# Four edits to a two-branch encoder layer: gated copies, 2 KB rows for an intermediate, an engine pinned for some splits, and attention scores in runs of four blocks

## The chip, the cores and the metric

The kernel runs on 1 core of one Trainium2 chip. The metric is the device time of one execution in microseconds, taken over several executions. One core has five instruction streams: TensorE (PE in the profile; its weight loads are PEld), VectorE (DVE), ScalarE (ACT), GpSimd (POOL) and SyncE (SP), which here issues every DMA. All DMAs of this kernel go through SyncE's one queue and are carried out by 16 DMA engines. On chip there are SBUF (128 partitions) and PSUM (eight banks of 128 x 512 float32, which TensorE writes and VectorE and ScalarE read).

## What is computed

One encoder layer is applied to two inputs, a prompt of 512 tokens and a sample of 1024 tokens, with shared weights; the model width is 1024.

```python
h = rmsnorm(x, norm_g)
qa, ka, va, za, qb, kb, vb, zb, ga, gb = split(h @ w_in)       # 1024 x 5376
oa = neighbourhood_attention(norm(qa), norm(ka), va, rpb_a) * silu(za)   # branch A: 8 heads of 64, 8 x 16 window on a grid 64 wide
oa = oa @ w_o_a                                                # 512 x 1024
ob = window_gqa_attention(norm(qb), norm(kb), vb, t5_table, sink_b) * silu(zb)  # branch B: 8 heads, 2 key heads, |i-j| <= 128
ob = ob @ w_o_b
y = x + (sigmoid(ga) * oa + sigmoid(gb) * ob) @ w_out
```

Everything is float32. The kernel keeps that accuracy by splitting each operand of a matmul into a high part (rounded to the matrix engine's float32 format) and a low part (the difference), and by adding three products: high x high, high x low, low x high. ScalarE makes a high part by a copy; VectorE or GpSimd makes the low part by a subtraction.

## The kernel before

**Stages.** First comes the prompt's attention (`attention_phase`), then the prompt's dense phase (`dense_phase`: the gates z and g, the two projections back to width 1024, the merge, the output), then the same two for the sample. Within the trace the prompt's attention lies at about 10 to 215 us, its dense phase up to about 395, the sample's attention from there to about 786, the sample's dense phase after that.

**Order of the work.** Nothing is ordered by hand. Every instruction or small group is an `Op` of the class `Flow`, with a list of engines that may do it and an assumed duration on each, a priority `prio` (smaller is earlier), values that it makes, uses or fills (`new`, `use`, `into`, `hold`), and other operations that it comes after. `Flow.run` is a list scheduler in Python that simulates the engines with the assumed durations while the program is built, and emits instructions in the order in which it would start them. Each engine then works through its own fixed stream on the chip. An operation that has both VectorE and GpSimd among its choices goes to the one that would end it first, and is marked `port`: the planner doesn't start a marked operation on one of the two engines while a marked one runs on the other. An operation with VectorE alone is not marked unless it says so. A DMA is assumed to take 470 ns of SyncE's queue and then a time by its bytes. A value belongs to a rotation of `bufs` buffers, and a new one waits until the oldest is free. `f.begun[nt, prio]` is the first matmul of the projection with that priority.

**Attention.** The heads are done in six groups: branch A as four groups of two heads (`gi` 0 to 3), branch B as two groups of four query heads and one key head. Priorities rise by one for each tile of 128 tokens: the projection of tile `t` in group `gi` has `prio = gi * nb + t`, with `nb` = 4 tiles for the prompt and 8 for the sample. `project` (L764) makes 384 columns of q, k, v of one tile by 24 matmuls into a PSUM bank of the two with the tag `p`; the squares' sums (`ss`, VectorE), the reciprocal root (`rs_v` and `rs_r`, GpSimd) and the scaled q and k (`qk`, VectorE) follow, then TensorE transposes `qk` (L864) and ScalarE and VectorE write `kt` and `qt`. For branch B the rows of h are first copied to the buffers `hb` in natural order of tokens (L665 and L667, four copies of 128 x 512 a tile, on ScalarE or VectorE; four buffers, so one tile's copies are in flight at a time).

`attend` (L937) computes scores. It takes a batch of blocks of 128 queries, two blocks for branch A and one for branch B, and gives each block's head a whole PSUM bank of the five with the tag `x`. A pair of heads lies on partitions 0 to 63 and 64 to 127, so score matmuls use 64 rows of the array each. In the prompt a block of branch A has 256 keys. Prompt's four blocks of branch A cover tiles (0, 1), (1, 2), (2, 3) and, for both ends of the sequence, (0, 3). `weigh` then adds the bias and takes the maximum on VectorE (L972), the exponential on ScalarE (L981), scales, transposes on TensorE (L1029), splits into `pp` (L1035, L1040), multiplies by `v` (L1066) and stores the outcome `ot`. The rotation of `v` has six buffers for the prompt.

A block's outcome goes to the DRAM tensor `o_d`. For branch B the block's 128 queries are every `nb`-th column of h's order, so `post_z` reads `o_d` back in pieces: for a half of 512 columns of the sample, 128 partitions x 8 blocks x 64 columns, 256 bytes a piece.

**Fill-in.** `fill_gates` takes some gate products (weights `fr`, split into `fh` and `fl`, PSUM bank with the tag `d`) at a late priority, so that TensorE has work where attention has none ready.

**Dense phase of the sample.** Most products of two pairs of weight chunks with two halves of h are done by a scheme with seven products instead of eight (`pair_strassen`), which multiplies sums of weights (`S`) with sums of h. h's sums are made early, stored in DRAM as `t_d`, and read back by `stored_sums` at the start of the phase into `U`, `fh` and `w32`, from which `split` makes the high and low parts `T` (L1172 on ScalarE, L1177 on VectorE or GpSimd). L1293 to L1295 are the three products. `post_z` multiplies silu(z) with what attention left; its loads are L1535, the store of the result `u_d` is L1520.

Of the kernel before, what the change touches and what calls it, by code (L numbers as in the profile page):

```python
# [10 lines left out]
F32 = mybir.dt.float32  # L11
# [15 lines left out]
SLACK = 1.1  # L27
SCRATCH = 1024
# [12 lines left out]
P = 128  # L41
# [313 lines left out]
def encoder_kernel(  # L355
# [23 lines left out]
    nc = tc.nc  # L379
# [24 lines left out]
    o_d = {geo.nt: dpool.tile([2, 8, P, geo.nt], F32, tag=f"o_d{geo.nt}", name=f"o_d{geo.nt}") for geo in (gp, gs)}  # L404
# [246 lines left out]
    def attention_phase(geo, hh, hl, h_ops, mask_d, early, late):  # L651
# [79 lines left out]
        def project(br, w, t, prio):  # L731
# [10 lines left out]
            else:  # L742
# [6 lines left out]
                for q in range(2):  # L749
                    for m, v in enumerate((hh, hl)):  # L750
# [5 lines left out]
                            prio - 1, new=[hb[m][q]], hold=[v], after=[o for u in h_ops.values() for o in u], port=True,  # L756
# [154 lines left out]
        def attend(br, gi, g, batch, nb_t, info, prio):  # L911

            nh = 2 if br == "A" else 4
            k0 = 2 * (gi % 2)
            states = []
            for block in batch:
                sums = tuple(tile_([P, 4], F32, tag, 3) for tag in ("mx", "sm", "rs", "es"))
                pss = [bank("x") for _ in range(nh)]
# [7 lines left out]
            def emit(e):  # L926

                for block, _, pss, _ in states:
                    runs, tiles, width, step, whole = places(block)
                    q = queries(block)  # L930
                    for pair in range(nh // 2):
                        at = runs[0][0] if whole else pair * P
                        for n, (u, k) in enumerate(((0, 0), (0, 1), (1, 0))):
                            for i in range(2):
                                rows = slice(64 * i, 64 * i + 64)
                                kv = kt.t[rows, k0 + k].rearrange("p (t n) -> p t n", n=P)
                                pe.matmul(  # L937
                                    pss[2 * pair + i].t[:, :width], q.t[rows, u, at : at + P],
# [3 lines left out]
            def queries(block):  # L942
# [5 lines left out]
                (("pe", ns),), emit, prio, new=[v for _, _, pss, sbs in states for v in (*pss, *sbs)],  # L948
# [12 lines left out]
        def weigh(br, gi, g, block, sums, pss, sbs, nb_t, info, prio):  # L961
# [7 lines left out]
            def score(i, ps, sb):  # L969
                def emit(e, i=i, ps=ps, sb=sb):  # L970
                    init = 3.0e38 if br == "A" else nsink[:, 4 * g + i : 4 * g + i + 1]
                    dve.tensor_tensor_reduce(  # L972
                        out=sb.t[:, :width], in0=ps.t[:, :width], in1=bias_of(br, nb_t, i, table), scale=1.0,
# [18 lines left out]
            for i, (ps, sb) in enumerate(zip(pss, sbs)):  # L992
                score(i, ps, sb)
# [82 lines left out]
            if br == "A":  # L1076
# [10 lines left out]
                def emit():  # L1087
                    if len(runs) == 1:
                        dst = over(o_d[nt][0, g], runs).rearrange("(i p) n -> p i n", i=2)
                        nc.sync.dma_start(dst, ot.t[:64, ::2])  # L1090
                        return
                    for i in range(2):
                        dst = over(o_d[nt][0, g, 64 * i : 64 * i + 64], runs)
# [3 lines left out]
            else:  # L1097
                for e in range(2):
                    dst = o_d[nt][e, 4 + 2 * g : 6 + 2 * g, :, runs[0][0] : runs[0][0] + P]
                    dst = dst.rearrange("c (i d) n -> d (c i) n", d=64)  # L1100
                    o = sp(
                        lambda e=e, dst=dst: nc.sync.dma_start(dst, ot.t[e * 64 : e * 64 + 64]),
                        131072, prio, use=[ot],
                    )
                    for c in (4 + 2 * g, 5 + 2 * g):
# [848 lines left out]
```

## Time and profile before

| | us |
|---|---|
| median of 3 runs | 1133.49 |
| lowest, highest | 1132.47, 1138.85 |
| profiled execution | 1135.29 |
| its span, first to last instruction | 1133.5 |
| TensorE busy | 1119.0 (99%) |
| VectorE busy | 860.1 (76%) |
| ScalarE busy | 651.9 (58%) |
| GpSimd busy | 337.3 (30%) |

Busy time of TensorE counts an instruction from its start to its modelled end, and matmuls overlap in the pipeline: a busy TensorE can still be slower than it might be. The rows of the profile name an instruction by engine, line of the kernel, and out<-in with the program's tile names (`w` stands for `w32`). All times of rows are from the span's start.

### The profile page before, as it was taken

How to read it: one execution, taken by the hardware profiler on the slowest of the kernel's cores; microseconds unless marked ns; L12 is line 12 of the kernel's file. 1: busy time of each engine (PE TensorE's matmuls, PEld its weight loads, DVE VectorE, ACT ScalarE, POOL GpSimd, SP SyncE). 2: the span in 40 equal slices, each digit the busy share in tenths (PEclk: the TensorE clock that was granted, in tenths of full speed). 3: DMA queues.
4: the chain of work that ended last, by engine and by line, in shares of the span. 5: the costliest groups of instructions: out<-in, count | busy, mean ns of one | idle time of the engine just before them, and what ended most of it. 6: DMA issues, size and time to landing. Idle time of an engine off the chain costs nothing.

```text
span 1133.5 us, 18690 instructions
## 1 busy us (share of the span) xinstructions
PE 1119.0 (99%) x6079; PEld 973.2 (86%) x6079; DVE 860.1 (76%) x1988; ACT 651.9 (58%) x1499; POOL 337.3 (30%) x438
## 2 busy tenths in 40 slices
PE   8999999999999999999999999999999999999998
PEld 6999988888888889999999988988788888888887
DVE  5888797587776568787878888885988766677764
ACT  6777987644432257565769888876543335423430
POOL 4653433000011154434324344420333322222211
PEclk9999999999999999999999999999999999999999
DMA  7854543488886732121212314244977645867862
GB/s 263 276 155 138 184 115 103 110 257 248 256 278 216 254 128 91 27 63 30 82 41 85 81 38 112 57 131 121 307 241 234 224 156 170 281 207 222 280 215 93
DMA packets 139108, 186.11 MB, mean 164 GB/s; under 512 B 29897, under 2 KB 68561, under 8 KB 139010
## 3 DMA queue, kind: packets, MB, share of 16 engines
q1 hardware_dynamic: 139010, 184.91, 51.8%
q8 instruction: 48, 0.79, 0.3%
q14 instruction: 50, 0.41, 0.1%
HBM read 137.66 MB, written 51.92 MB: 167 GB/s over the span
## 4 chain that ended last, share of the span: by engine, by line
PE 93%; DMA 2%; DVE 2%; issue 1%; ACT 1%; POOL 1%; SPq 0%; DVEq 0%; ACTq 0%
PE p L764 25%; PE x L1294 9%; PE x L1295 9%; PE x L1293 9%; PE x L1066 5%; PE x L937 5%; PE x L1029 5%; PE d L1293 4%; PE d L1295 4%; PE d L1294 4%; PE p L1294 4%; PE p L1295 4%; PE p L1293 4%; PE x L864 2%; DMA w<-in_w_att_dram 1%
## 5 line engine op out<-in xcount | busy, mean ns | idle before, releaser
L764 PE MATMUL p<-whi,hh 128*128 128x384 f32 x384 | 133.4, 348 | 0.0
L764 PE MATMUL p<-whi,hl 128*128 128x384 f32 x384 | 132.2, 344 | 0.0
L764 PE MATMUL p<-wlo,hh 128*128 128x384 f32 x384 | 131.8, 343 | 0.0
L1172 ACT ACTIVATE whi<-raw 128x512 fp32r<-128x512 f32 (+1 forms) x140 | 81.4, 600 | 71.2 <-PE x L1294 22.3
L981 ACT ACTIVATE sb<-sb,mx 128x384 f32<-128x384 f32 (+1 forms) x192 | 107.8, 565 | 16.9 <-DVE mx L972 16.5
L1295 PE MATMUL x<-T,wlo 128*128 128x512 f32 x280 | 108.9, 389 | 0.0
L1294 PE MATMUL x<-T,whi 128*128 128x512 f32 x280 | 108.9, 389 | 0.0
L1293 PE MATMUL x<-T,whi 128*128 128x512 f32 x280 | 108.9, 389 | 0.0
L764 PE MATMUL p<-whi,hb 128*128 128x384 f32 x384 | 107.6, 346 | 0.0
L1177 POOL TENSOR_TENSOR wlo<-raw,whi 128x512 fp32r<-128x512 f32 (+1 forms) x33 | 39.5, 1204 | 215.6 <-DMA raw<-in_w_g_dram 112.9
L1040 DVE TENSOR_TENSOR pp<-x,pp 128x512 fp32r<-128x512 f32 (+1 forms) x136 | 82.5, 638 | 19.6 <-ACT pp L1035 19.0
L1177 DVE TENSOR_TENSOR wlo<-raw,whi 128x512 fp32r<-128x512 f32 (+1 forms) x107 | 72.0, 682 | 32.3 <-ACT whi L1172 28.7
L802 POOL TENSOR_TENSOR rs_r<-rs_v,mhalf 128x4 f32<-128x4 f32 (+1 forms) x72 | 80.5, 1118 | 5.7
L1035 ACT ACTIVATE pp<-x 128x512 fp32r<-128x512 f32 (+1 forms) x136 | 70.8, 559 | 15.8 <-PE x L1029 14.3
L1294 PE MATMUL x<-hl,whi 128*128 128x512 f32 x200 | 77.8, 389 | 0.0
L1295 PE MATMUL x<-hh,wlo 128*128 128x512 f32 x200 | 77.8, 389 | 0.0
L1293 PE MATMUL x<-hh,whi 128*128 128x512 f32 x200 | 77.8, 389 | 0.0
L1066 PE MATMUL x<-pp,v 128*128 128x256 f32 (+1 forms) x368 | 75.8, 322 | 0.0
L764 PEld LDWEIGHTS p<-whi,hl 128*128 128x128 f32 x384 | 72.6, 189 | 1.3 <-issue 1.0
L764 PEld LDWEIGHTS p<-wlo,hh 128*128 128x128 f32 x384 | 72.7, 189 | 1.0 <-issue 0.7
L764 PEld LDWEIGHTS p<-whi,hh 128*128 128x128 f32 x384 | 72.7, 189 | 0.7 <-DVE v L812 0.3
L764 PEld LDWEIGHTS p<-whi,hb 128*128 128x128 f32 x384 | 69.1, 188 | 3.1 <-issue 1.3
(388 smaller groups left out, 2965.1 us busy)
## 6 DMA issues: line engine op xcount, KB each, us to landing
raw<-in_w_g_dram SPq DMA_DIRECT2D x84, 256.0 KB
w<-in_w_att_dram SPq DMA_DIRECT2D x46, 384.0 KB
raw<-in_w_z_dram SPq DMA_DIRECT2D x40, 256.0 KB
ot<-o_d SPq DMA_DIRECT2D x36, 256.0 KB
g_d<-C SPq DMA_DIRECT2D x34, 256.0 KB
fr<-in_w_g_dram SPq DMA_DIRECT2D x28, 256.0 KB
raw<-in_w_out_dram SPq DMA_DIRECT2D x28, 256.0 KB
out_dram<-C SPq DMA_DIRECT2D x19, 256.0 KB
```

What stands on the lines that cost most here:

```text
L764: pe.matmul(ps.t[:, :GW], part[u](k), mv.t[:, c], start=k == 0 and m == 0, stop=k == KC - 1 and m == 2,)
L802: lambda e: nc.gpsimd.tensor_tensor(r.t[:, :nn], rv.t[:, :nn], mhalf[:, :nn], op=ALU.pow),
L937: pe.matmul(pss[2 * pair + i].t[:, :width], q.t[rows, u, at : at + P], kv[:, tiles[0] : tiles[-1] + 1 : step], start=n == 0, stop=n == 2,)
L981: act.activation(sb.t[:, :width], sb.t[:, :width], AF.Exp, bias=mx.t[:, i : i + 1], scale=-1.0, accum_out=sm.t[:, i : i + 1],)
L1035: lambda e, pt=pt, pp=pp, nn=nn: act.activation(pp.t[:, 0, :nn], pt.t[:, :nn], AF.Copy),
L1040: lambda e, pt=pt, pp=pp, nn=nn: dve.tensor_tensor(pp.t[:, 1, :nn], pt.t[:, :nn], pp.t[:, 0, :nn].bitcast(F32), op=ALU.subtract),
L1066: pe.matmul(out(), v.t[:, vs], mv(), start=first, stop=last)
L1172: (("act", ACT_(n)),), lambda e: act.activation(hi(), src(), AF.Copy), prio,
L1177: lambda e: engines[e].tensor_tensor(lo(), src(), hi().bitcast(F32), op=ALU.subtract), prio,
L1293: pe.matmul(out, hi.t[:, cs], mh(), start=first and k == 0, stop=False, **more)
L1294: pe.matmul(out, hi.t[:, cs], ml(), start=False, stop=False, **more)
L1295: pe.matmul(out, lo.t[:, cs], mh(), start=False, stop=last and k == len(ws) - 1, **more)
```

## The change

Four edits are made at once.

1. The copies to `hb` of branch B also wait for the beginning of the projection that is six tiles earlier (`AHEAD = 6`).
2. Branch A's outcome stays in `o_d`, without its unused second half. Branch B's goes to a tensor of its own, `ob_d`, in which 512 columns of h's order lie together, the blocks one after the other. A block's store is made separately for each half of the sequence (four DMAs in the sample instead of two, in pieces of 256 bytes instead of 512; in the prompt two as before, in pieces of 512 bytes), and the load in `post_z` reads rows of 2 KB.
3. In the sample, the low parts of h's sums and of the first pair's weights (`prio` 0) have VectorE as their only choice; before, they had VectorE or GpSimd.
4. In the prompt, branch A's scores are taken in batches of four blocks instead of two. The second block of each pair gets columns 256 to 511 of the first one's banks.

```diff
+AHEAD = 6
...
-    o_d = {geo.nt: dpool.tile([2, 8, P, geo.nt], F32, ...) for geo in (gp, gs)}
+    o_d = {geo.nt: dpool.tile([4, P, geo.nt], F32, ...) for geo in (gp, gs)}
+    ob_d = {geo.nt: dpool.tile([geo.nt // 512, 2, 8, 64, 512], F32, ...) for geo in (gp, gs)}
...
@@ project
-                            prio - 1, new=[hb[m][q]], hold=[v], after=[o for u in h_ops.values() for o in u], port=True,
+                            prio - 1, new=[hb[m][q]], hold=[v], port=True,
+                            after=[*(o for u in h_ops.values() for o in u), f.begun[nt, prio - AHEAD]],
...
@@ attend
+            shared = br == "A" and nt == NT_P
...
-                pss = [bank("x") for _ in range(nh)]
+                second = shared and len(states) % 2
+                pss = [(v, 256) for v, _ in states[-1][2]] if second else [(bank("x"), 0) for _ in range(nh)]
...
+                                ps, a = pss[2 * pair + i]
                                 pe.matmul(
-                                    pss[2 * pair + i].t[:, :width], q.t[rows, u, at : at + P],
+                                    ps.t[:, a : a + width], q.t[rows, u, at : at + P],
...
@@ weigh (stores of branch B)
-                for e in range(2):
-                    dst = o_d[nt][e, 4 + 2 * g : 6 + 2 * g, :, runs[0][0] : runs[0][0] + P]
-                    dst = dst.rearrange("c (i d) n -> d (c i) n", d=64)
-                    o = sp(
-                        lambda e=e, dst=dst: nc.sync.dma_start(dst, ot.t[e * 64 : e * 64 + 64]),
-                        131072, prio, use=[ot],
-                    )
+                m, t = 512 // nb, runs[0][0] // P
+                for n in range(nt // 512):
+                    for e in range(2):
+                        dst = ob_d[nt][n, e, 4 * g : 4 * g + 4, :, t * m : t * m + m].rearrange("a p m -> p a m")
+                        o = sp(
+                            lambda n=n, e=e, dst=dst: nc.sync.dma_start(dst, ot.t[e * 64 : e * 64 + 64, :, n * m : n * m + m]),
+                            1024 * m, prio, use=[ot],
+                        )
...
-                size = 2 if br == "A" else 1
+                size = 1 if br == "B" else 4 if nt == NT_P else 2
...
@@ split (b is the low part)
-                any_tt(n),
+                any_tt(n)[: 1 + both],
...
@@ stored_sums
-                        (vh, k == 0), (vl, k == 0), [st],
+                        (vh, k == 0), (vl, k == 0), [st], both=d is m_d,
...
@@ pair_strassen
-            w = weight_tiles([*first, s2, s3, s1, raw[1, 1], s4], 6, prio - 0.5)
+            w = weight_tiles([*first, s2, s3, s1, raw[1, 1], s4], 6, prio - 0.5, prio > 0)
...
@@ post_z
-                    src, dst = o_d[nt][e, c, :, a : a + n], lambda ot=ot: ot.t[:, :n]
+                    src = o_d[nt][c, :, a : a + n]
                 else:
-                    src = o_d[nt][e, c].rearrange("p (i n) -> p i n", n=P)[:, :, a // nb : a // nb + m]
-                    dst = lambda ot=ot: ot.t[:, :n].rearrange("p (i n) -> p i n", n=m)
+                    src = ob_d[nt][a // nh, e].rearrange("(c i) p n -> c (i p) n", i=2)[c - 4, :, :n]
```

`any_tt(n)` is `(("dve", ...), ("pool", ...))`, so `any_tt(n)[:1]` leaves VectorE alone. `split` and `weight_tiles` take `both=True` where nothing is given.

More of the change, by code (lines that the diff above doesn't have):

```diff
@@ L403, in encoder_kernel @@
     t_d = dpool.tile([4, 4, P, NT_S // 2], F32, tag="t_d", name="t_d")
-    o_d = {geo.nt: dpool.tile([2, 8, P, geo.nt], F32, tag=f"o_d{geo.nt}", name=f"o_d{geo.nt}") for geo in (gp, gs)}
+    o_d = {geo.nt: dpool.tile([4, P, geo.nt], F32, tag=f"o_d{geo.nt}", name=f"o_d{geo.nt}") for geo in (gp, gs)}
+    ob_d = {geo.nt: dpool.tile([geo.nt // 512, 2, 8, 64, 512], F32, tag=f"ob_d{geo.nt}", name=f"ob_d{geo.nt}") for geo in (gp, gs)}
     s_d = dpool.tile([4, 4, P, 512], F32, tag="s_d", name="s_d")
@@ L947, in attend @@
             o = f.op(
-                (("pe", ns),), emit, prio, new=[v for _, _, pss, sbs in states for v in (*pss, *sbs)],
+                (("pe", ns),), emit, prio, new=[v for _, _, pss, sbs in states for v in (*(ps for ps, a in pss if not a), *sbs)],
                 use=[queries(block) for block in batch], after=[o for b in batch for t in b[1] for o in info[t][2]],
@@ L967, in weigh, with score, emit @@
             mx, sm, rs, es = sums
-            def score(i, ps, sb):
-                def emit(e, i=i, ps=ps, sb=sb):
+            def score(i, ps, a, sb):
+                def emit(e, i=i, ps=ps, a=a, sb=sb):
                     init = 3.0e38 if br == "A" else nsink[:, 4 * g + i : 4 * g + i + 1]
                     dve.tensor_tensor_reduce(
-                        out=sb.t[:, :width], in0=ps.t[:, :width], in1=bias_of(br, nb_t, i, table), scale=1.0,
+                        out=sb.t[:, :width], in0=ps.t[:, a : a + width], in1=bias_of(br, nb_t, i, table), scale=1.0,
                         scalar=init, op0=ALU.add, op1=ALU.min, accum_out=mx.t[:, i : i + 1],
@@ L990, in score @@
                 x.vals = [*x.vals, mx]
-            for i, (ps, sb) in enumerate(zip(pss, sbs)):
-                score(i, ps, sb)
+            for i, ((ps, a), sb) in enumerate(zip(pss, sbs)):
+                score(i, ps, a, sb)
             if br == "B":
@@ L1088, in emit @@
                     if len(runs) == 1:
-                        dst = over(o_d[nt][0, g], runs).rearrange("(i p) n -> p i n", i=2)
+                        dst = over(o_d[nt][g], runs).rearrange("(i p) n -> p i n", i=2)
                         nc.sync.dma_start(dst, ot.t[:64, ::2])
@@ L1092, in emit @@
                     for i in range(2):
-                        dst = over(o_d[nt][0, g, 64 * i : 64 * i + 64], runs)
+                        dst = over(o_d[nt][g, 64 * i : 64 * i + 64], runs)
                         nc.sync.dma_start(dst, ot.t[:64, 2 * i].rearrange("p (a b) -> p a b", b=64))
@@ L1097, in weigh @@
             else:
[L1098 to L1106 removed]
+                m, t = 512 // nb, runs[0][0] // P
[6 more added lines that the diff above has]
+                        )
+                        for c in (4 + 2 * g, 5 + 2 * g):
                             stores[c, n].append(o)
@@ L1166, in tt, with split @@
             return f.op(choice, lambda e: engines[e].tensor_tensor(out(), in0(), in1(), op=op), prio, **kw)
-        def split(hi, lo, src, n, prio, new_hi, new_lo, src_v, after=()):
+        def split(hi, lo, src, n, prio, new_hi, new_lo, src_v, after=(), both=True):
             kw = lambda v, new: {"hold": [v]} if new is None else {"new": [v]} if new else {"into": [v]}
@@ L1258, in load_raw, with weight_tiles @@
             return v
-        def weight_tiles(operands, per, prio):
+        def weight_tiles(operands, per, prio, both=True):
             n = -(-len(operands) * 4 // per)
@@ L1275, in weight_tiles @@
                         lambda src=src, sc=sc: src.t[:, sc], m * P, prio,
-                        (hi, ti not in seen), (lo, ti not in seen), [src],
+                        (hi, ti not in seen), (lo, ti not in seen), [src], both=both,
                     )
```

3 lines of the change are left out of this document (1 added, 2 removed).

## Prediction

> **What bounds the kernel now.** I read the page first: shares of busy time, then TensorE's waits, then busy time by stretch, then the order of instructions around each wait.
>
> ```profile
> span 1133.5 us, 18690 instructions
> PE 1119.0 (99%) x6079; PEld 973.2 (86%) x6079; DVE 860.1 (76%) x1988; ACT 651.9 (58%) x1499; POOL 337.3 (30%) x438
> ```
>
> TensorE is busy for all but 14.5 us of the span, so an edit pays only where it removes one of TensorE's waits or shortens TensorE's own stream. The change removes no matmul. The view of waits, for TensorE alone, says what there is to win:
>
> ```profile
> PE x L864 <- DVE qk L819: 3.1, 3, 1.8
> PE d L1294 <- DVE T L1177: 1.6, 1, 1.6
> PE p L1294 <- DVE T L1177: 0.9, 2, 0.7
> ```
>
> The columns are who waited, for whom, us in total, times, longest. The rows not shown lie before the first projections, which the change leaves alone, but for the smallest one. The first one shown has its longest part at the sample's first attention tile; the two with T are the start of the sample's dense phase. Busy time by stretch places both (after the length, 30.00: busy PE, PEld, DVE, ACT, POOL, each with its count, the clock, the DMA engines' share, GB/s):
>
> ```profile
> 390.00:420.00 30.00, 28.16 (x160) 25.95 (x159) 18.76 (x48) 12.36 (x26) 11.48 (x16) 1.00 0.59 195
> 690.00:720.00 30.00, 30.00 (x191) 26.71 (x190) 25.23 (x69) 25.56 (x65) 11.06 (x15) 1.00 0.40 111
> 810.00:840.00 30.00, 27.53 (x119) 21.83 (x118) 29.76 (x42) 11.77 (x24) 12.83 (x9) 1.00 0.76 253
> ```
>
> TensorE is idle for 1.84 us in the first, for none in the middle one (branch B of the sample, DMA engines at 0.40), for 2.47 us in the last, where VectorE is busy for 29.76 of 30. The granted clock is 1.00, so no term comes from the clock.
>
> **Part 1: prompt's branch A scores, runs of four.** Score matmuls use 64 rows, those around them 128. The row of the tile of queries, one of the chain (start, us, what) and TensorE's timeline (start, us to the end of the last, engine, line) show what a run costs:
>
> ```profile
> L937 PE MATMUL x<-kt,qt x96: 271/278/384, 38.5 to 127.6; 64*128 64x256 f32 x96
> 39.80 4.18 PE p L764 x24
> 126.64 0.34 PE L764 MATMUL p<-wlo,hb 128*128 128x384 f32 x1
> 126.91 0.97 PE L937 MATMUL x<-kt,qt 64*128 64x256 f32 x12
> 127.81 0.62 PE L764 MATMUL p<-whi,hb 128*128 128x384 f32 x2
> 128.28 0.34 PE L764 MATMUL p<-wlo,hb 128*128 128x384 f32 x1
> ```
>
> A tile's 24 projection matmuls take 4.18 us, 0.174 each. From 126.64 to 128.28 are 1.64 us, in which three of them (0.52) and twelve scores start. The twelve are six pairs, and I take the two of a pair to go side by side on the two halves of the rows, or 0.90 us would not hold them: at 256 of 384 columns a pair is 0.174 x 2/3 = 0.116, six are 0.70. The rest, 0.42 us, is the price of entering and leaving the 64-row form. 96 matmuls in twelves are 8 runs; in twenty-fours they are 4. Removed: 4 x 0.42 = 1.7 us of TensorE's stream, which nothing hides because TensorE is never idle there.
>
> Against it stands a later softmax. The first two blocks used to start at the third tile, now all four start at the fourth:
>
> ```profile
> 63.87 0.97 PE L937 MATMUL x<-kt,qt 64*128 64x256 f32 x12
> ...
> 74.02 0.63 PE L1066 MATMUL x<-pp,v 128*128 128x256 f32 x4
> L972 DVE CUSTOM_DVE_ANT_0 sb<-x,bias 128x256 f32<-128x256 f32 x16 | 5.8, 418 | 0.3 <-PE x L937 0.3
> ```
>
> Two blocks take 63.87 to 74.65, 10.8 us, from first score to last product. Two more put four scores ahead on VectorE, 4 x 0.42 = 1.7 us, and as much again for the later steps: my estimate is 14 us. Behind it TensorE has the next group's four projections, 4 x 4.18 = 16.7 us, and fill-in gate products. The cover ends at the six `v` buffers: the next group's third tile needs the buffer of this group's first, which the block of both ends reads last; two PSUM banks of projections still go on. So it holds, with under 3 us to spare. Two blocks in one bank also let VectorE begin only after the second block's pairs if the wait is by bank, 3 x 0.116 = 0.35 us, hidden likewise. Bounds: -1.7, and +1.5 if the softmax outlasts its cover by 1 us at each of three boundaries; I take -1.5, near the row, with a little for the thin cover.
>
> **Part 2: branch B's copies later.** The gate holds only a batch's first four copies; the others wait for the four `hb` buffers as before. In the prompt the four lie after the first projections, where TensorE's waits name no copy: nothing gained. In the sample they lie in the wait:
>
> ```profile
> 402.04 2.46 ACT L665 ACTIVATE hb<-hh 128x512 fp32r<-128x512 f32 x2
> 402.62 2.15 DVE L667 CAST hb<-hl 128x512 fp32r<-128x512 f32 x2
> 402.23 1.31 POOL L1177 TENSOR_TENSOR fl<-fr,fh 128x512 fp32r<-128x512 f32 x1 [11.40 <-ACT fh L1172]
> 403.62 1.22 POOL L795 TENSOR_SCALAR rs_v<-ss 128x4 f32<-128x4 f32 x1
> 406.02 0.19 POOL L795 TENSOR_SCALAR rs_v<-ss 128x4 f32<-128x4 f32 x1
> 406.45 0.44 PE L864 MATMUL x<-ident,qk 128*128 128x128 f32 x2 [1.84 <-DVE qk L819]
> ```
>
> TensorE waits for `qk`, which waits for the reciprocal roots on GpSimd. `rs_v` took 1.22 us beside the copies on VectorE, 0.19 us without them: 1.03 us. Before it GpSimd did a fill-in weight's low part for 1.31 us, which VectorE, free of 2.15 us of copies, may take instead; then the whole 1.84 us go. Bounds 0 (another late step in its place) and -1.84; I take -1.4, between the two mechanisms. The copies then run up to six tiles ahead of their use, between other work of both engines and beside a TensorE with projections to do: nothing there, and if that cover were gone ScalarE's 2.46 us.
>
> **Part 3: branch B's outputs as 2 KB rows, and h's sums on VectorE.** These meet at 790 to 821. The queue's and the engines' timelines, and two rows of the chain:
>
> ```profile
> 791.71 2.14 SPq L1535 DMA_DIRECT2D ot<-o_d  x2
> 793.90 3.66 SPq L1520 DMA_DIRECT2D u_d<-C  x1
> 798.13 2.69 DMA U<-t_d
> 803.77 6.24 DMA ot<-o_d
> 810.10 1.25 DVE L1166 TENSOR_TENSOR ot<-ot 128x512 f32<-128x512 f32 x1 [0.46 <-DMA ot<-o_d]
> 811.27 1.75 DVE L1177 TENSOR_TENSOR T<-w,T 128x512 fp32r<-128x512 f32 x1
> 810.76 1.71 POOL L1177 TENSOR_TENSOR wlo<-raw,whi 128x512 fp32r<-128x512 f32 x1
> 813.08 0.50 PE L1294 MATMUL d<-T,whi 128*128 128x512 f32 x1 [1.57 <-DVE T L1177]
> 813.41 0.40 PE L1295 MATMUL d<-T,wlo 128*128 128x512 f32 x1
> ```
>
> An `ot` load of 256 KB in 256-byte pieces took 6.24 us of the chain, a `U` load of the same size in 2 KB rows 2.69. Behind two such loads the queue's next issue, one store, stood for 3.66 us, and the loads of h's sums (`U` at 798.13) queued behind that store. VectorE then stood 0.46 us for `ot`, with the `T` that TensorE wanted behind it. With 2 KB rows the piece count of a load falls from 1024 to 128, so both delays should go. TensorE's waits for `T` are three, 1.6 + 0.9 = 2.5 us in the view of waits. In an undisturbed stream (the last two rows of the next fence) a product starts 0.22 us after the one before, which ends 0.39 after its start: the idle mark leaves 0.17 us of each wait out, and the restart is slow by 0.11 (813.08 to 813.41). 2.5 + 3 x 0.28 = 3.3 us. `T` and the first pair's low weights on VectorE alone cost it one more `T` at most there, 0.68 us less what it no longer loses beside GpSimd.
>
> Against it: the stores. A sample block now issues four stores in 256-byte pieces instead of two in 512-byte ones.
>
> ```profile
> q1 hardware_dynamic: 602, 0.35, 50.7%
> 785.75 1.24 SPq L1102 DMA_DIRECT2D o_d<-ot__10494  x2
> 788.18 0.42 SPq L1245 DMA_DIRECT2D U<-t_d  x1
> 796.04 0.68 DVE L1177 TENSOR_TENSOR T<-fh,T 128x512 fp32r<-128x512 f32 x1
> 797.88 0.39 PE L1293 MATMUL x<-T,whi 128*128 128x512 f32 x1
> 798.10 0.39 PE L1294 MATMUL x<-T,whi 128*128 128x512 f32 x1
> ```
>
> The first row is the DMA view of 781.8 to 785: 602 packets, 512 of them a block's stores, held the engines for 50.7% of 3.2 us, 1.6 us. Twice the packets cost between nothing (same bytes) and 1.6 us more per block. Through branch B that is hidden by DMA engines at 0.40, and the queue's two more issues a block (1.24 us) by TensorE's work. Only the last two blocks, the later one issued at 785.75, push the first `U` load at 788.18: 2 x 1.24 us of issue and up to 3.2 us of transfer. The second `T` is ready at 796.72 for a product at 797.88: 1.16 us of slack. Bounds of part 3: -3.3, and +1.3 (2.5 us late less the slack, nothing won); I take -2.3, nearer to the first, since the `ot` load is what the chain names.
>
> On small pieces the Trainium skill (DMA: Bandwidth & Descriptors, Specifications) holds 512 bytes to be the least for line rate, with read-modify-write below. No run here shows a 256-byte store; by that rule a block's stores would take at least the upper bound and part 3 would be near -0.7, by 1.6 us for the last block.
>
> **Sum.** -1.5 - 1.4 - 2.3 = -5.2 us. The sum is made on a span of 1133.5 (that execution took 1135.29 with what lies around it, 1.8 us over the median of the three runs, 1133.49). Put on the median: 1128.3 us, 0.46% faster. 0.5%, 5.7 us, is about what a measurement of this kernel can tell from no change.
>
> **Rivals.** *All three in full*: -1.7 - 1.84 - 3.3, 1126.6, and 1125.4 if the new order also spares the other 3.1 - 1.84 = 1.26 us before `L864`; for it speaks that each wait is named after what the change moves. *The stores take back the loads' gain*: parts 1 and 2, -2.9, and part 3 at +0.4 between its ends: 1131.0. *VectorE meets GpSimd*: a split that has VectorE as its only choice is no longer kept apart from GpSimd's by the planner; `T` took 1.75 us beside GpSimd's 1.71 and 0.68 alone, so two such meetings on the path cost 2 x 1.07 us and part 3 comes to -0.2: 1130.4. The Trainium skill (SBUF — State Buffer, SBUF: two separate sides) calls the shared ports an exclusive lock held for an instruction; the slow `T` agrees. *Slower*: the four-block softmax outlasts its cover. Past 16.7 us each us is idle at three group boundaries; at 20.4 us, 11.1 us are lost and the time is 1139.4, 0.5% slower. Against it, two blocks take 10.8.
>
> **Chances.** Forecast 0.43 (1127 to 1130), all in full 0.23, stores 0.16, VectorE meets GpSimd 0.11, slower 0.07. Under 1127.8 lie the second and some 0.17 of the first: faster 0.40, same 0.53, slower 0.07. Range 1125.5 to 1132.5, which leaves out the slow case and the edges of the others.
>
> **What would show it.** Part 1: 4 runs of 24 score matmuls in the prompt and no TensorE wait before 200 us that wasn't there. Part 2: no `hb` near 400, `rs_v` at about 0.2 us, the wait for `qk` under 0.7 us. Part 3: `ot` loads landing in about 3 us, no store issue of 3.6 us, TensorE's waits for `T` under 1 us in all. Wrong it would be if new TensorE waits show in the prompt's A groups, at 797, or where the planner's other order puts them.

## The result: 0.63% slower

| | before | after |
|---|---|---|
| median, us | 1134.47 (6 runs) | 1141.81 (6 runs) |
| lowest, highest | 1132.47, 1140.47 | 1140.77, 1144.74 |
| profiled execution, its span | 1135.29, 1133.5 | 1142.45, 1140.7 |

The ratio is 1.0063, with an interval of 1.0043 to 1.0083: 7.1 us slower, where 5.2 us faster was forecast. The profiled execution of after (1142.45 us) lies near the median (1141.81), so its trace can be read for the loss. First its page and the view of waits for TensorE (who waited, for whom, us in total, times, longest):

```profile
span 1140.7 us, 18743 instructions
PE 1122.9 (98%) x6079; PEld 975.0 (85%) x6079; DVE 854.5 (75%) x1959; ACT 653.5 (57%) x1502; POOL 358.4 (31%) x464
PE x L867 <- DVE qk L822: 3.5, 3, 2.7
PE d L1300 <- DVE T L1183: 2.2, 3, 0.7
PE d L1299 <- ACT fc L1621: 1.8, 4, 0.7
PE p L1300 <- DVE T L1183: 1.1, 2, 0.7
PE x L1299 <- ACT fl L1653: 0.4, 1, 0.4
```

Neither of the two waits that the change was to shorten is shorter: `qk` 3.5 us (3.1 before), `T` 3.3 us (2.5). GpSimd is busier by 21 us, VectorE less busy by 6. The stretches by windows, the last one shifted by 3 us, as TensorE's first wait for `T` is (813.08 before, 815.98 after):

```profile
390.00:420.00 30.00, 27.01 (x138) 25.04 (x137) 14.08 (x33) 8.10 (x20) 9.86 (x14) 0.94 0.59 193
690.00:720.00 30.00, 30.00 (x195) 26.97 (x192) 25.45 (x72) 25.42 (x64) 10.51 (x15) 1.00 0.47 107
813.00:843.00 30.00, 26.60 (x112) 20.08 (x111) 28.29 (x37) 11.83 (x24) 15.73 (x12) 1.00 0.68 223
```

In the first, VectorE has 4.7 us less to do, and yet TensorE idles 2.99 us instead of 1.84 and the granted clock is 0.94. In the last, TensorE idles 3.40 us, and GpSimd is busy for 15.73 us instead of 12.83.

Where the span went is best seen from five lengths, worked out from starts in TensorE's timeline of each kernel's profiled execution: to the first projection; the prompt (to the sample's first projection); the sample's attention (to the last product with `v`); the start of its dense phase (to 4 us behind the 121st matmul with `T`); the rest. The kernels below the line are those of the experiments.

| us | to first projection | prompt | sample's attention | dense start | rest |
|---|---|---|---|---|---|
| before | 11.0 | 383.0 | 390.7 | 55.5 | 293.3 |
| after | 10.2 | 384.9 | 394.2 | 58.2 | 293.3 |
| | | | | | |
| gate alone | 10.3 | 384.5 | 389.9 | 57.3 | 293.3 |
| rows alone | 10.3 | 383.4 | 390.2 | 51.9 | 294.0 |
| VectorE splits alone | 10.3 | 382.8 | 390.7 | 56.8 | 293.3 |
| runs of four alone | 10.4 | 387.6 | 390.0 | 54.0 | 293.3 |
| all but the gate | 10.3 | 387.7 | 390.8 | 57.3 | 293.3 |
| all but the VectorE splits | 10.2 | 386.4 | 391.4 | 52.6 | 293.3 |
| after + seat | 10.4 | 385.0 | 391.0 | 57.4 | 293.3 |
| after + later bias | 10.8 | 383.2 | 391.2 | 58.2 | 293.3 |
| after + port mark | 10.6 | 385.3 | 392.3 | 54.4 | 293.3 |
| three mends | 10.6 | 385.3 | 391.0 | 53.8 | 293.3 |
| three mends, no runs of four | 10.3 | 384.5 | 389.9 | 53.9 | 293.3 |
| tuned rows | 10.3 | 382.9 | 388.3 | 52.2 | 293.3 |

Of the 7.2 us between the two spans, -0.9 lies before the first projection, +1.9 in the prompt, +3.5 in the sample's attention, +2.7 in the dense start.

How far a single execution can be trusted is seen from kernels whose traces have the same order of instructions on TensorE, VectorE, ScalarE and GpSimd. In the prompt these are after, all but the VectorE splits, seat, later bias, port mark and the three mends: they take 383.2 to 386.4 us. In the sample's attention they are after, all but the VectorE splits, seat and port mark: 391.0 to 394.2 us, and after's is the highest. So a difference of 1 or 2 us in these two columns says little where it stands alone.

**The sample's first tiles.** TensorE, VectorE, GpSimd and SyncE in time order (start, us, engine, line; in brackets the idle time and what ended it):

```profile
401.73 1.19 SPq L676 DMA_DIRECT2D mask<-in_mask_s_dram  x1
404.10 0.20 POOL L798 TENSOR_SCALAR rs_v<-ss 128x4 f32<-128x4 f32 x1
405.91 0.44 PE L867 MATMUL x<-ident,qk 128*128 128x128 f32 x2 [0.31 <-DVE qk L822]
408.71 1.49 DVE L700 TENSOR_TENSOR bias<-mask,raw 128x192 f32<-128x192 f32 x5 [2.66 <-DMA mask<-in_mask_s_dram]
410.13 0.41 DVE L822 TENSOR_TENSOR qk<-p,rs_r 128x256 f32<-128x256 f32 x1
410.59 0.44 PE L867 MATMUL x<-ident,qk 128*128 128x128 f32 x2 [2.68 <-DVE qk L822]
411.92 0.51 PE L767 MATMUL p<-whi,hh 128*128 128x384 f32 x1
412.22 0.52 PE L767 MATMUL p<-wlo,hh 128*128 128x384 f32 x1
415.38 0.33 PE L767 MATMUL p<-whi,hl 128*128 128x384 f32 x1
```

No copy to `hb` is left here, `rs_v` takes 0.20 us, and the first wait for `qk` is 0.31 us. But what VectorE does next in its stream is the bias table, which needs the mask, and that hasn't landed. VectorE stands 2.66 us with the second tile's `qk` behind it, and TensorE as long. (Before, the bias table stood in front of that `qk` as well, at 406.51, but VectorE didn't stand for the mask.) From 411.92 matmuls then start 0.28 to 0.32 us apart instead of 0.17, until 415.38: 1.5 us more.

**The dense start.** ScalarE, SyncE, GpSimd, VectorE and TensorE:

```profile
790.25 2.56 SPq L1109 DMA_DIRECT2D ob_d<-ot__10510  x4
794.47 1.28 ACT L1519 ACT_TABLE_LOAD   x1 [2.85 <-DMA ob_d<-ot__10510]
799.42 1.05 SPq L1540 DMA_DIRECT2D ot<-ob_d  x2
800.59 0.42 SPq L1526 DMA_DIRECT2D u_d<-C  x1
809.76 5.62 POOL L1183 TENSOR_TENSOR wlo<-S,whi 128x512 fp32r<-128x512 f32 x4 [8.03 <-ACT whi L1178]
809.54 0.68 DVE L1183 TENSOR_TENSOR T<-fh,T 128x512 fp32r<-128x512 f32 x1
810.62 1.30 DVE L1183 TENSOR_TENSOR T<-U,T 128x512 fp32r<-128x512 f32 x1 [0.40 <-ACT T L1178]
815.84 1.77 DVE L1183 TENSOR_TENSOR T<-U,T 128x512 fp32r<-128x512 f32 x1
817.54 1.77 DVE L1183 TENSOR_TENSOR T<-w,T 128x512 fp32r<-128x512 f32 x1
817.67 0.50 PE L1300 MATMUL d<-T,whi 128*128 128x512 f32 x1 [0.73 <-DVE T L1183]
```

The queue is as forecast: two loads of `ot` are issued in 1.05 us, and the store of `u_d` behind them in 0.42. When these loads land is not on record, but from 785 to 830 no engine waits for one, where VectorE and GpSimd stood 5.7 us for such loads before. Two things are new. ScalarE's first gate waits 2.85 us for the last stores of branch B. And the low parts of `T`, on VectorE alone now, take up to 1.77 us beside GpSimd's `wlo` and its sums `S`, where one without company takes 0.68; TensorE waits for `T` five times. Eight of the eleven from 809.5 to 827 are longer than 0.9 us, together by 5.9 us.

### The profile page after: what moved, and what is told of

The parts are those of the page before. It is cut to its first block, busy times and chain, and to the rows that moved or that the text cites. A ratio compares the mean times of both kernels' runs of the same rounds, so it can differ in the third digit from the quotient of the medians.

```text
span 1140.7 us, 18743 instructions
## 1 busy us (share of the span) xinstructions
PE 1122.9 (98%) x6079; PEld 975.0 (85%) x6079; DVE 854.5 (75%) x1959; ACT 653.5 (57%) x1502; POOL 358.4 (31%) x464
## 4 chain that ended last, share of the span: by engine, by line
PE 76%; DMA 9%; DVE 8%; issue 3%; ACT 2%; SPq 1%; POOL 1%; DVEq 0%; ACTq 0%; POOLq 0%
PE p L767 25%; PE x L1300 6%; PE x L1299 6%; PE x L1301 6%; PE x L1072 5%; PE x L943 5%; PE x L1035 4%; PE d L1299 3%; PE d L1301 3%; PE d L1300 3%; PE p L1300 3%; PE p L1299 3%; PE p L1301 3%; PE x L867 2%; DVE wlo L1183 2%
## 5 line engine op out<-in xcount | busy, mean ns | idle before, releaser
L987 ACT ACTIVATE sb<-sb,mx 128x384 f32<-128x384 f32 (+1 forms) x192 | 107.6, 564 | 12.5 <-DVE mx L978 11.9
L1183 POOL TENSOR_TENSOR wlo<-raw,whi 128x512 fp32r<-128x512 f32 (+1 forms) x35 | 42.5, 1220 | 217.9 <-ACT whi L1178 213.4
L767 PE MATMUL p<-whi,hb 128*128 128x384 f32 x384 | 110.1, 348 | 0.0
L1183 DVE TENSOR_TENSOR wlo<-raw,whi 128x512 fp32r<-128x512 f32 (+1 forms) x105 | 74.6, 718 | 36.6 <-ACT whi L1178 27.8
```

The lines of the kernel that those rows point to most:

```text
L767: pe.matmul(ps.t[:, :GW], part[u](k), mv.t[:, c], start=k == 0 and m == 0, stop=k == KC - 1 and m == 2,)
L987: act.activation(sb.t[:, :width], sb.t[:, :width], AF.Exp, bias=mx.t[:, i : i + 1], scale=-1.0, accum_out=sm.t[:, i : i + 1],)
L1183: lambda e: engines[e].tensor_tensor(lo(), src(), hi().bitcast(F32), op=ALU.subtract), prio,
```

## Experiments

Ratios are to the kernel before, with 95% intervals. The first four kernels make one edit each.

**Gate alone.**

```diff
+AHEAD = 6
-    prio - 1, new=[hb[m][q]], hold=[v], after=[o for u in h_ops.values() for o in u], port=True,
+    prio - 1, new=[hb[m][q]], hold=[v], port=True,
+    after=[*(o for u in h_ops.values() for o in u), f.begun[nt, prio - AHEAD]],
```

> The kernel before with the gate on branch B's copies alone. Theory 1 (the wait moves on): with the copies gone, TensorE's wait for the sample's first qk (1.84 us) falls under 0.6, but VectorE then reaches the first bias before the mask's load has landed, the second tile's qk stands behind it, TensorE idles 2 to 3 us and then runs some 3 us at half clock (320 ns a projection matmul instead of 174): 1 to 3 us slower than before. Theory 2 (the mask is late only because of the other three edits): the first wait falls and none follows, 1 to 2 us faster. Theory 3 (the planner's new order spreads the loss anywhere): waits appear at places the copies don't touch, and this spot shows nothing of the kind.

Measured: 1.0021 [1.0008, 1.0034]. The wait for the first `qk` is gone, and the second tile waits 1.35 us instead (VectorE stood 1.48 us for the mask): 0.8 us won in the sample's attention. The prompt is 1.5 us longer. The dense start is 1.8 us longer: ScalarE's table load waits for the last block's store here too:

```profile
788.95 1.28 ACT L1515 ACT_TABLE_LOAD   x1 [1.89 <-DMA o_d<-ot__10494]
```

No edit touched that gate. A buffer gets its place in the attention's pool when it is first made. The gated `hb` (four buffers, 8 KB a partition) are first made behind `ot_` instead of ahead of it, so `ot_` lies 8 KB lower, where the next stage's first result goes, and ScalarE waits until what lay there has been stored. Theory 1 named the right place in the sample, but the second tile's wait is shorter than its 2 to 3 us, no half clock follows (the granted clock is 1.00 from 390 to 420), and the loss lies elsewhere: in the prompt and in the dense start.

**Rows of 2 KB alone.** The new `ob_d`, its stores and loads:

```diff
-    src = o_d[nt][e, c].rearrange("p (i n) -> p i n", n=P)[:, :, a // nb : a // nb + m]
+    src = ob_d[nt][a // nh, e].rearrange("(c i) p n -> c (i p) n", i=2)[c - 4, :, :n]
```

> The kernel before with branch B's outputs as 2 KB rows alone. Theory 1 (stores): the last block's four stores take 2.5 us of the queue, ScalarE's first gate at the start of the sample's dense phase waits 2 to 3 us for a store to land before it may overwrite the block's memory, and every T comes later: TensorE's waits between 795 and 830 are at least as long as before (2.5 us) and the time is 0.5 to 3 us longer. Theory 2 (my forecast): ot loads land in about 3 us, the waits for T fall under 1 us, 2 us faster.

Measured: 0.9967 [0.9952, 0.9983]. The view of waits, in full behind the load at the very start:

```profile
PE x L865 <- DVE qk L820: 2.5, 4, 0.9
PE d L1294 <- ACT fc L1616: 0.2, 1, 0.2
PE x L1296 <- POOL wlo L1178: 0.2, 1, 0.2
PE x L1067 <- DVE pp L1041: 0.2, 1, 0.2
```

No wait for `T` is left and the dense start is 3.6 us shorter; the rest of the dense phase gives 0.7 us of it back (294.0 instead of 293.3). So the rows alone win 3.0 us in the dense phase, most of part 3's upper bound of 3.3. Theory 2 was right, and its 2 us too low: the ratio makes 3.7.

The stores cost TensorE nothing that shows. The first load of `U` is issued 4.8 us after the last product with `v` instead of 3.5, but the first product with `T` comes 12.5 us after it in both kernels, and from 690 to 720 TensorE is busy for 30.00 us, with the DMA engines at 0.45 instead of 0.40. What the stores cost the engines is in the DMA view: before, the 512 pieces of 512 bytes of a block take 1.4 us (544 packets, 69.6% of the 2.0 us from 782.9); here the 1024 pieces of 256 bytes take 1.7 us (1088 packets, 49.9% of the 3.4 us from 781.5).

**VectorE splits alone.**

```diff
-    any_tt(n),
+    any_tt(n)[: 1 + both],
```

(`both` false for h's sums in the sample, and for the weights of the first pair.)

> The kernel before with the low parts of h's sums and of the first pair's weights on VectorE alone. Theory 1 (VectorE meets GpSimd): at least four of the sixteen T splits run beside GpSimd work and take 1.2 to 1.8 us instead of 0.68; TensorE's waits for T grow from 2.5 to 4 us or more: 1 to 2 us slower. Theory 2 (my forecast): the same within 0.7 us, since a single T was on GpSimd before.

Measured: 1.0023 [1.0008, 1.0038]; dense start 1.3 us longer. Eight of the sixteen `T` take 0.98 to 1.78 us, each beside GpSimd, as theory 1 said; but TensorE's waits for `T` grow from 2.5 to 2.9 us only, not to the 4 it named.

**Runs of four alone.** `size = 4`, the second block of two in the upper half of the first one's banks.

> The kernel before with branch A's scores of the prompt in runs of four alone. Theory 1: eight entries into the 64-row form become four, 1.4 to 1.7 us less on TensorE, and new waits of the fill-in products for the single buffer fc near 125 and 146 us take about 1 us back: 0 to 1 us faster. Theory 2 (my forecast): no new wait, 1.5 us faster. Theory 3 (the planner's new order): waits also in the prompt's dense phase (near 355 and 385 us), 1 us or more slower.

Measured: 1.0019 [1.0007, 1.0032]. The runs came as drawn; these are the last one's neighbours in after, and new waits of the runs alone:

```profile
120.25 0.34 PE L767 MATMUL p<-whi,hb 128*128 128x384 f32 x1
120.52 1.70 PE L943 MATMUL x<-kt,qt 64*128 64x256 f32 x24
122.15 0.45 PE L767 MATMUL p<-whi,hb 128*128 128x384 f32 x1
122.43 0.34 PE L767 MATMUL p<-wlo,hb 128*128 128x384 f32 x1
...
64.62 0.44 PE L864 MATMUL x<-ident,qk 128*128 128x128 f32 x2 [1.79 <-DVE qk L819]
75.17 0.44 PE L864 MATMUL x<-ident,qk 128*128 128x128 f32 x2 [1.62 <-DVE qk L819]
```

and what stood ahead of both, on GpSimd and VectorE:

```profile
60.06 2.03 POOL L1180 TENSOR_TENSOR fl<-fr,fh 128x512 fp32r<-128x512 f32 x1
62.17 0.78 POOL L795 TENSOR_SCALAR rs_v<-ss 128x4 f32<-128x4 f32 x1
64.14 0.42 DVE L819 TENSOR_TENSOR qk<-p,rs_r 128x256 f32<-128x256 f32 x1 [0.91 <-POOL rs_r L802]
...
73.38 0.19 POOL L467 TENSOR_SCALAR nv<-ns 128x1 f32<-128x1 f32 x1 [1.58 <-ACT junk L463]
73.65 1.01 POOL L802 TENSOR_TENSOR rs_r<-rs_v,mhalf 128x4 f32<-128x4 f32 x1
```

From 120.25 to 122.43 are 2.18 us, less two projection matmuls (0.35) and twelve pairs (1.39): 0.44 us for one entry and exit. That is what a run of twelve cost (0.42), now four times instead of eight. Counted like this, from the matmul ahead of a run to the second one behind it, all runs of scores in the prompt, branch B's too, stand for 6.5 us before and 5.2 here (5.0 in after): 1.3 to 1.5 us of the 1.7 that were worked out.

Two waits for `qk`, 3.4 us, more than take it back, and the prompt is 4.6 us longer. Neither is the softmax's tail. At 64.14 `qk` stood for the reciprocal root, which came behind a fill-in weight's low part of 2.03 us on GpSimd. For the wait at 75.17 it stood for the root at 73.65, which in GpSimd's stream comes behind `nv`, an operation of the sample's norm that itself waited for ScalarE. Theory 3 was the nearest: two waits lie in the prompt's dense phase as it said (0.20 us at 357.70 and 1.01 at 386.65), but no theory named the waits for `qk`.

The four ratios add up to 1.0030, so half of the loss appears only in company. The next three runs take the changed kernel and mend one suspect each.

**Seat.**

```diff
+    seat = lambda: nt == NT_S and late.pool.tile([P, KC // 2, P], F32R, tag="hb", name="hb", bufs=HB)
-    sp(lambda: nc.sync.dma_start(mask.t, mask_d), 512 * at[-1], -0.5, new=[mask])
+    sp(lambda: (seat(), nc.sync.dma_start(mask.t, mask_d)), 512 * at[-1], -0.5, new=[mask])
```

> The changed kernel with one thing more: in the sample, the pool of branch A and B's tiles gets its room for hb (8 KB per partition) laid down where the kernel before had it, right behind raw and mask, instead of behind ot_. No instruction is added, and the order on every engine is the changed kernel's. Theory 1 (the later copies moved ot_ down by 8 KB, so that ScalarE's first gate of the sample's dense part writes where the last ot_ of branch B still lies, and has to wait until its four stores have landed: 2.85 us at 794.47): the table load waits for no DMA and starts about 3 us earlier, at 0.2 us after what stands before it, and TensorE's waits in the first 58 us of the dense part fall from 5.3 us to 2 to 3.5; the time is about 2 us below the changed kernel's, 1.0045 of the kernel before (1.0035 to 1.0055). Rival (these waits come from VectorE's splits beside GpSimd, and ScalarE has slack): the table load moves, the waits stay above 4.8 us, 1.006. The start of the sample's attention is the same in both: a wait of 2.7 us and a stretch at half clock near 411.

Measured: 1.0051 [1.0032, 1.0069]. The table load waits for nothing, and the waits in the dense start (TensorE's idle time there, and for each wait the 0.17 us that the idle mark leaves out) fall only from 5.3 to 4.5 us:

```profile
788.77 1.28 ACT L1519 ACT_TABLE_LOAD   x1
```

So the store is real and worth 0.8 us; theory 1 fails for the rest. The order of instructions is after's own on every engine, yet the sample's attention takes 391.0 us and not 394.2. TensorE waits 2.08 us at the first tile (for a reciprocal root behind a fill-in's low part that takes GpSimd 1.29 us at 404.87), 0.47 us at the second, and the clock stays at 1.00. So most of after's 3.5 us in the sample's attention depends on when the mask and the weights land in an execution (at 402.99 ScalarE had stood 2.38 us for weights here).

**Later bias.** The first bias table takes its place behind the second tile's `qk`:

```diff
-    nb_t = tables(br, g, lead - 1)
+    nb_t = None if gi == 0 and nt == NT_S else tables(br, g, lead - 1)
...
+    nb_t = nb_t or t and (mask.writers.append(qk.writers[0]), tables(br, g, lead - 1))[1]
```

> The changed kernel, with the bias table of the sample's first group of branch A computed after the scaled q and k of the second tile instead of before them. Theory 1 (the wait that took the place of the hb copies: VectorE stands 2.66 us at the addition that needs the mask, q and k of the second tile stand behind it, TensorE idles 2.68 us at 410.6 and then runs 11 matmuls at half clock, 1.5 us): the wait for qk falls to 0.3 to 1.0 us, the spacing of the 128x384 matmuls stays at 174 ns from 405 to 420, the sample's attention takes 391.0 us and not 394.4; about 3.4 us below the changed kernel, 1.0033 of the kernel before (1.0023 to 1.0045). Rival (the mask is what is late, not the order): the first scores now wait for the bias, which cannot be ready before the mask lands near 408.3, and 2 of the 2.7 us come back as a wait at the first scores; 1.0055 or more. The waits at the start of the dense part (5.3 us) stay in both, unless the planner's order changes there.

Measured: 1.0036 [1.0023, 1.0048]. No half clock, no wait for the second tile, and no new one at the first scores; what is left is 1.74 us at the first tile (406.35). The sample's attention is 3.0 us shorter than after's, the dense start the same 58.2. That is as theory 1 said, but for the 1.74 us where it had 1.0 at most. How much of it is the edit's is not settled: seat, without this edit, has an attention as short, and the interval of the ratio touches after's (1.0043).

**Port mark.**

```diff
-    use=src_v, after=[a, *after], **{**kw(*new_lo), ...},
+    use=src_v, after=[a, *after], port=True, **{**kw(*new_lo), ...},
```

> The changed kernel, with the low-part subtraction of every split marked as one that takes the shared port again (in the changed kernel those that only VectorE may do had lost the mark, so the planner set them beside GpSimd's). Theory 2 (VectorE meets GpSimd: T's low parts take 1.2 to 1.8 us beside GpSimd's and 0.68 alone): they take 0.68 to 0.8 us, TensorE's waits in the first 58 us of the sample's dense part fall from 5.3 to 2.5 to 3.8 us, about 2 us below the changed kernel, 1.0045 of the kernel before. Rival a (the store that ScalarE waits for sets them): T's low parts are short, the waits stay above 4.8 us, 1.006. Rival b: held back from VectorE's time, GpSimd's weight splits come late, and TensorE waits for wlo instead; 1.006 to 1.008.

Measured: 1.0024 [1.0011, 1.0037]. The waits for `T`:

```profile
PE p L1300 <- DVE T L1183: 1.2, 2, 1.0
```

1.2 us instead of 3.3, the dense start 3.8 us shorter, though the store still holds ScalarE for 2.85 us. This is theory 2, and more than it said in time; three of the `T` still take 1.18 to 1.79 us, beside GpSimd's `S`.

**All but the gate, all but the VectorE splits.**

> The changed kernel without the gate on branch B's copies (parts 1 and 3 alone: runs of four, rows of 2 KB, h's sums on VectorE). Theory 1 (the gate is what costs most in company: the wait behind the mask with the half clock, 4.2 us, and the store that ScalarE waits for, about 2 us, both of which appear only where the other parts make the stretch tighter): the first wait is the old one, 1 to 2 us without half clock, the first gate waits for no store, T's waits are under 3 us; 1.0010 of the kernel before (0.9995 to 1.0025), which is less than the changed kernel by more than the gate alone costs (0.0021). Rival (the four parts add up, and what is over is the order's chance): 1.0042, the changed kernel less the gate's 0.0021.

Measured: 1.0046 [1.0032, 1.0060]: the rival's number. The dense start is 57.3, without any late store; the prompt is 387.7, as with the runs alone. Theory 1 fell: the gate isn't the dearest part. The runs of four have their two waits again (1.80 us at 64.35, 1.07 at 74.39), which no kernel with the gate shows.

> The changed kernel without the restriction to VectorE (h's sums and their weights may be split on GpSimd again, as before). ScalarE's first gate still has to wait for the last four stores of branch B. Theory 1 (the late store sets the dense part's waits): the table load still waits near 2.9 us, and TensorE's waits in the first 58 us of the sample's dense part stay at 3 us or more; 1.0045 of the kernel before or more. Theory 2 (VectorE's splits beside GpSimd set them; the rows of 2 KB alone had no wait left there): the table load waits 2.9 us just the same, the waits for T fall from 5.3 us below 1, the first 58 us of the dense part come down by 4 to 6 us, 1.0010 to 1.0028 of the kernel before. What remains above 1 is the start of the sample's attention and the prompt.

Measured: 1.0005 [0.9989, 1.0020], 6.6 us below the changed kernel: of the two parts taken out of it, this one costs far more. These rows have everything in them:

```profile
411.72 0.44 PE L867 MATMUL x<-ident,qk 128*128 128x128 f32 x2 [2.78 <-DVE qk L822]
413.04 0.33 PE L767 MATMUL p<-whi,hh 128*128 128x384 f32 x1
413.22 0.33 PE L767 MATMUL p<-wlo,hh 128*128 128x384 f32 x1
793.18 1.28 ACT L1519 ACT_TABLE_LOAD   x1 [2.85 <-DMA ob_d<-ot__10510]
809.89 0.69 DVE L1183 TENSOR_TENSOR T<-w,T 128x512 fp32r<-128x512 f32 x1
810.76 3.71 POOL L1183 TENSOR_TENSOR wlo<-S,whi 128x512 fp32r<-128x512 f32 x1 [31.63 <-ACT whi L1178]
```

ScalarE waits its 2.85 us, GpSimd does one `wlo` before 814, `T` takes 0.69 us, and TensorE waits for `T` nowhere, as theory 2 said. Where the two engines still meet it is GpSimd that pays: its `wlo` stands 3.71 us beside four `T`, and TensorE doesn't wait for it. And TensorE idles 2.78 us behind the mask, a little longer than in after, with no half clock behind it.

**Three mends together, with and without the runs of four.**

> The changed kernel with all three mends together: hb's room where it was, the first bias table behind the second tile's q and k, the splits marked for the shared port. If the three costs stand beside one another, the gains of the single runs add: 1.0063 less 0.0012, 0.0027 and 0.0039, so 0.9985 of the kernel before (0.997 to 1.0005), with under 1.5 us of waits in the first 58 us of the dense part and no half clock near 411. Rival (the prompt carries a loss of its own, from the runs of four): those waits are gone as said and the time is still above 1.002, with the prompt 2 us or more longer than before between its first projection and its end (384.5 us and not 382.5).

Measured: 0.9999 [0.9981, 1.0016]; no half clock, waits in the dense start 1.7 us, a little over the 1.5 said. The prompt is 2.3 us longer than before, as the rival has it, but the time is below its 1.002 and in the first theory's range: the three costs stand beside one another, as far as the interval tells.

> The changed kernel with the three mends and without the runs of four (branch A's scores in the prompt in runs of two blocks, a bank each). Theory 1 (the runs of four take 1.4 us of row switches off and pay more than that back: fill that waits for ScalarE, waits for q and k, in all 2 us in the prompt): the switch term of the prompt goes back from 4.85 to 6.25 us, its waits fall to 0.7 us, and the kernel is 0 to 2 us faster than the one with the three mends alone; 0.996 to 0.998. Rival (the runs of four are worth their 1.4 us, the rest is scatter): 1 to 1.5 us slower than the mends alone, 0.9985 to 1.0005.

Measured: 1.0002 [0.9990, 1.0015], not to be told from the former, so theory 1's 0.996 to 0.998 is missed. The entries and exits went back to 6.4 us; the prompt is 384.5 instead of 385.3. Both kernels with a gate and without the runs of four have this 384.5, 1 to 1.7 us more than the four with neither (382.8 to 383.4); 0.5 us of it is a wait of a projection from `hb` (at 144.0 here, 145.1 in the gate alone) for VectorE's `v`.

**Tuned rows.** Rows, seat, later bias, and the gate in the sample only (`f.begun[nt, prio - AHEAD] if nt == NT_S else None`).

> A version made from the runs so far: the rows of 2 KB (0.9967 alone), the gate on branch B's copies in the sample only, hb's room where it was, the first bias table behind the second tile's q and k; neither runs of four nor the restriction to VectorE. Theory 1 (with the mask out of the way, the copies' place is free to be won): TensorE's waits at the start of the sample's attention fall from 1.3 to 0.3 to 0.8 us, no wait for T; 0.9955 to 0.9967 of the kernel before. Rival (the mask lands at its time whatever stands ahead of it, and the first scores wait instead): 0.9967 to 0.998, no faster than the rows alone.

Measured: 0.9962 [0.9945, 0.9978], median 1130.44, faster than both kernels. Its profiled execution shows no TensorE wait at the sample's first tiles, and the bias table runs after both `qk`:

```profile
403.59 0.38 PE L867 MATMUL x<-ident,qk 128*128 128x128 f32 x2
404.87 0.42 PE L867 MATMUL x<-ident,qk 128*128 128x128 f32 x2
```

That is 1.9 us off the sample's attention against the rows alone in the profiles; the intervals of the two overlap, so the times don't show it.

## Why the prediction was wrong

Between the -5.2 us of the forecast and the measured +7.1 lie 12.3. Taken alone, the four edits cost +2.4 us (gate), -3.7 (rows), +2.6 (splits) and +2.2 (runs of four), by their ratios: 3.4 in all, which is 8.6 of the 12.3. The other 3.7 appear only in company.

**Part 1 (-1.5): its gain right, the planner's new order left out.** The row switches gave 1.3 to 1.5 us. "No TensorE wait before 200 us that wasn't there" failed: after has waits for `fc` of 0.69 us at 125.37 and 0.34 at 146.14, the runs alone 3.4 us for `qk`. The slower rival was right about the place, the prompt, but not about the mechanism. The waits for `qk` are for reciprocal roots that GpSimd reached late; at 125.37 a new fill-in product stands right behind the last one and has to wait until ScalarE has copied that one out of the bank `d` (0.60 us from 124.72). No wait of TensorE's in the prompt of these two kernels names a step of the softmax. Net, with the gate, it is worth nothing that can be measured (0.9999 and 1.0002).

**Part 2 (-1.4): the copies' step right, the next late things not named.** There is no `hb` near 400, and `rs_v` takes 0.20 us, as said. The 0.31 us for `qk` belong to this execution: seat, with the same order, waits 2.08 us there, since the fill-in's low part stayed on GpSimd, where the prediction let VectorE take it. The bound of 0, "another late step in its place", was left without a name: it was the mask's load, there 7 us after its issue, with the bias table that needs it in front of the second `qk` in VectorE's stream. The gate alone kept 0.8 us. In after the stretch lost 3.5, 1.5 of them by the half clock, for which the prediction had "no term"; in the three other kernels with this order it lost 0.3 to 1.6. Two costs were outside the working: 1.5 us in the prompt, where "nothing gained" was written and nothing lost was meant, and the moved `ot_`, 0.8 us.

**Part 3 (-2.3): the rows right, the VectorE splits mis-sized.** The rows alone brought the dense phase down by 3.0 us, near the bound of 3.3. The stores were put at nothing to 1.6 us more a block; they took 0.3 us more of the DMA engines and nothing of TensorE. Rows of 2 KB don't make a load short by themselves, as 2.69 against 6.24 us suggested: two loads of `t_d` stand for 5.37 and 5.06 us in after's chain (from 797.20 and 805.37), where the DMA engines are busy all the time from 799 to 806. By the Trainium skill's rule on pieces below 512 bytes (DMA: Bandwidth & Descriptors, Specifications) part 3 would have been near -0.7; the 0.3 us don't bear that out.

The step that failed is "`T` and the first pair's low weights on VectorE alone cost it one more `T` at most there, 0.68 us less what it no longer loses beside GpSimd". The opposite happened. Without the mark, the planner set GpSimd's `wlo` and `S` next to VectorE's `T`, and eight of eleven `T` took 5.9 us more than alone. From 52.6 us without the splits to 58.2 with them, it cost 5.6 us in the dense start: the rows' gain and 2 us more. The mark alone brings 3.8 of the 5.6 back (54.4 us); the other 1.8 stay while VectorE is the only choice. The rival "VectorE meets GpSimd" had the mechanism with the right reason, at two meetings of 1.07 us and a chance of 0.11. The Trainium skill (SBUF — State Buffer, SBUF: two separate sides) has the loser of the shared ports block for an instruction; 1.77 us beside GpSimd's 1.73 and 0.68 alone agree.

The sum took the three parts to stand beside one another. Rows and splits go for the same wait: once the rows had removed it, the splits had nothing to win there and only their price was left.

## What to carry to other kernels

Two edits aimed at one wait don't add: cost the second against the trace as the first leaves it. When an operation's list of engines is cut, look at what the scheduler read from that list; here the cut also dropped the mark that kept two engines apart. When something is moved out of a wait, name the next instruction in that engine's stream and what it needs, and ask whether a later first use moves a buffer onto memory that a transfer still reads. And before a difference of a few us in one stage is given a cause, compare executions that have the same order of work.

## What was not expected of the hardware

Of two idle times of TensorE at the same place, 2.68 us (after) was followed by a stretch at half speed and 2.78 us (all but the VectorE splits) by none. The windows of after (behind the busy times the granted clock, the DMA engines' share, GB/s):

```profile
410.00:412.00 2.00, 1.41 (x9) 1.41 (x10) 1.33 (x6) 0.63 (x2) 0.00 (x0) 0.98 0.25 77
412.00:414.00 2.00, 2.00 (x8) 2.00 (x7) 1.64 (x7) 0.00 (x0) 0.78 (x1) 0.50 0.06 22
414.00:416.00 2.00, 2.00 (x10) 2.00 (x9) 0.83 (x4) 0.55 (x2) 0.05 (x1) 0.67 0.26 58
```

At half speed these clocks mean 0.08, 2.00 and 1.32 us, 3.4 us in all. The length of the gap alone doesn't decide. The Trainium skill (TensorE: Matmul & The Clock Gate, Part 1) describes a free-running window of about 3.4 us; the 3.4 us at half speed agree with its length, but an idle time shorter than the window was enough here. Which phase of the window each of the two gaps met, no run shows.

Nor is the half clock the change's alone. The granted clock over a whole execution lies below 1.00 (0.998 or 0.999) in 3 of the 6 of after, which took 1142.5 to 1144.7 us where the other three took 1140.8 to 1141.2, and in 23 of 84 of the kernel before that were measured beside the experiments. Where in those executions it fell, no trace shows.
